# Cross attention in a two-layer encoder step: each head's query projection in two halves of 128 features

## The chip, the cores and the metric

One core of a Trainium2 chip runs the whole step in one launch. The metric is the device time of one execution in microseconds. In the profile PE is TensorE (matmuls and transposes; the array runs its instructions in the order of its list), DVE is VectorE, ACT is ScalarE, POOL is GpSimd, SP issues the loads and stores.

## What is computed

Two layers for a prompt of 512 tokens and a sample of 32 tokens; 1024 features, each layer a mixer (differential attention and a gated part), cross attention with 4 heads of 256 features into 256 memory tokens, and a convolutional feed-forward part. The change lies in the cross attention:

```python
def mem_kv(mem, norm_g, wk, wv, kg):
    m = rmsnorm(mem, norm_g)
    k = rmsnorm((m @ wk).reshape(B, M, X_HEADS, X_DH), kg)
    v = (m @ wv).reshape(B, M, X_HEADS, X_DH)
    return k, v

def cross_attend(h, mk, mv, wq, wo, qg):
    q = rmsnorm((h @ wq).reshape(B, S, X_HEADS, X_DH), qg)
    s = jnp.einsum('bqhd,bkhd->bhqk', q, mk,
                   preferred_element_type=jnp.float32) * (X_DH ** -0.5)
    p = jax.nn.softmax(s, axis=-1)
    o = jnp.einsum('bhqk,bkhd->bqhd', p.astype(mv.dtype), mv).reshape(B, S, D_MODEL)
    return o @ wo
```

The prompt attends to memory keys and values computed here, the sample to cached ones.

## The kernel before

Prompt and sample stand side by side as 544 columns (`T`), in two PSUM tiles of 272. Every large product is made of three matmuls per block of 128 x 128 weights, high part by high, high by low and low by high, in a 32-bit format whose rounded high part and remainder are kept apart (`split`: ACT casts the high part, DVE subtracts it).

Weights come as a list of items (`build_units`), and the code must take them (`pop`) in the order of that list. An item is loaded by SP into one of two staging tiles `raw` and converted into a pair of tiles `hl` (ACT the high part, L192; DVE the rest, L193), eight tiles in all, so four items. A head's query weights `wq` are two items here, 512 input rows by 256 columns each.

The cross attention of a head h is, in the order of the code: `do_mem_k` (keys from wk: PSUM tile `pm`; squares and their sums; a reciprocal root on POOL, `rmk`; the scaled keys `mk` on DVE; transposes `pmk` on PE; the cached keys' transposes `pcmk`), `do_cross_q` (queries, PSUM tiles `pqa` and `pqb` in `proj_fm`, L353, 48 matmuls for each 128 features; squares `xsq`; their sums by a small product `pqs`; the reciprocal root on POOL, `rqy`, and from it `rq` and `nrq` on DVE), `do_cross_scores` (scores `pxS`, L940, 24 matmuls in two halves of 12; their maxima `xmx` on DVE; the exponentials `P` on ACT, L949; the division on DVE, L953; the transposes `pxT` of `P`, L960, split by ACT and DVE into `pT`; for the sample the scores `pxs`, L967, which take a PSUM bank that the first half of `pxS` has, and the transposes `pxsT`, L979), `do_mem_v` (values from wv, again `pm`, then `mv` and its split `mvs`), `do_cross_out` (`pxo` and `pxso`, the results `co`). For head 0 the queries come ahead of the keys. After the four heads wo's projection (`pwca`, `pwcb`, in the same `proj_fm`) adds to the residual; the part that takes heads 0 to 2 can run before the last head's result is there.

PSUM has four banks for `pm`, `pq` and `pwc`, two for `pxS` and `pxs`, two for the transposes and `pxo`.

The code is written in this order, but the order on each engine is not: a scheduler of the tile framework sets it at build time, by its own estimate of when each instruction can start, and mixes what is written one behind the other. Each engine then runs its own list in order and waits where a semaphore isn't there yet.

Of the kernel before, what the change touches and what calls it, by code (L numbers as in the profile page):

```python
# [10 lines left out]
F32R = mybir.dt.float32r  # L11
I32 = mybir.dt.int32
AF = mybir.ActivationFunctionType
# [14 lines left out]
T = 544  # L28
S0 = 512
TH = T // 2  # L30
# [6 lines left out]
def encoder_step(ctx: ExitStack, tc: tile.TileContext, a, o):  # L37
# [20 lines left out]
    def G(tag, shape, name, dt=F32):  # L58
        return gp.tile(shape, dt, tag=tag, bufs=GB[tag], name=name)

    def tmp(shape, name, tag="t", bufs=5, dt=F32):
        return tp.tile(shape, dt, tag=tag, bufs=bufs, name=name)
# [28 lines left out]
    for i in range(NP):  # L91
        q = i // PART - 1
# [7 lines left out]
    def build_units():  # L100
        def ks(src, k0, n):
            return src[k0 * 128:(k0 + n) * 128].rearrange("(k p) c -> p k c", p=128)

        def item(tag, what, ids, n):
            items.append((tag, what, ids, n))
            for r in ids:
                raws[r][2] = len(items) - 1

        def raw(loads, nk, cols, kind="raw"):
            raws.append([loads, nk, None, cols, kind])  # L110
            return len(raws) - 1

        def two(tag, mat, cols):
            for k0 in (0, 4):
                c0, loads = 0, []
                for c, n in cols:
                    loads.append((0, 4, c0, n, ks(mat[:, c:c + n], k0, 4)))
                    c0 += n
                item(tag, None, (raw(loads, 4, 256),), 4)

        for l in range(DEPTH):
            wi = a["w_in"][l]
            kq = lambda h: two(f"kq{h}", wi, [(512 + 128 * h, 128), (128 * h, 128)])
            v_ = lambda j: two(f"v{j}", wi, [(1024 + 256 * j, 256)])
            u_ = lambda j: two(f"u{j}", wi, [(1536 + 256 * j, 256)])
            gv = lambda j: two(f"gv{j}", wi, [(2048 + 256 * j, 256)])
            for f, i in ((kq, 0), (v_, 0), (kq, 1), (kq, 2), (v_, 1), (kq, 3), (gv, 0), (u_, 0), (gv, 1), (u_, 1)):
                f(i)
            for j in range(4):
                src = a["w_out"][l][:, 256 * j:256 * j + 256].rearrange("(b q k p) c -> q b p k c", b=2, q=2, p=128)  # L130
                for q in range(2):
                    item(f"wout{j}", None, (raw([(2 * b, 2, 0, 256, src[q, b]) for b in range(2)], 4, 256),), 4)
            for h in range(4):
                for nm in ("wq", "wk") if h == 0 else ("wk", "wq"):
                    two(f"{nm}{h}", a[nm + "_c"][l], [(256 * h, 256)])
                two(f"wv{h}", a["wv_c"][l], [(256 * h, 256)])
            for j in range(4):
                two(f"wo{j}", a["wo_c"][l], [(256 * j, 256)])

            ids = None  # L140
            for what, i, j in PLAN:
                if what != "d":
                    c0 = 256 * i + 128 * j + (FF if what == "u" else 0)
                    item(f"{what}{i}_{j}", None, (raw([(0, 8, 0, 128, ks(a["w_up"][l][:, c0:c0 + 128], 0, 8))], 8, 128),), 8)
                    continue
                jj, m = j // 7, j % 7
                if m == 0:
                    src = a["w_down"][l][256 * PART * i:256 * PART * (i + 1), 256 * jj:256 * jj + 256].rearrange(
                        "(k e p) c -> e p k c", e=2, p=128)
                    ids = [raw([(0, PART, 0, 256, src[e])], PART, 256, "rawb") for e in range(2)]  # L150
                item(f"d{i}_{jj}", SEVEN[m], ids, PART)
                raws[ids[0]][2] = min(raws[ids[0]][2], len(items) - 1 - max(0, m - 3))
            for j in range(4):
                n = NF - 2 * PART * NB
                item(f"dp{j}", None, (raw([(0, n, 0, 256, ks(a["w_down"][l][:, 256 * j:256 * j + 256], NF - n, n))], n, 256),), n)
# [71 lines left out]
    def pop(tag, n=2):  # L227

        for i in state.pop("done", ()):
            state["held"] -= cost(i)  # L230
        i = state["popped"]
        prefetch()
        res = []
        for j in range(i, i + n):
            assert items[j][0] == tag, (items[j], tag)
            res.append(wt.pop(j))
        state["popped"] = i + n
        state["done"] = range(i, i + n)
        return res
# [20 lines left out]
    def split(hi, lo, src):  # L260
        act.copy(hi, src)
        vec.tensor_tensor(out=lo, in0=src, in1=f32(hi), op=ALU.subtract)
# [36 lines left out]
    def halves(ps):  # L299
        return [(ps[i][:, 0:nn], n0, nn) for i, (n0, nn) in enumerate(NSPL)]  # L300

    def psR2(name, n=0):
        f = psS if n % 3 == 2 else psR
        return [f(name + "a"), f(name + "b")]
# [42 lines left out]
    def proj_fm(ps, col, parts):  # L347

        for hl, ks, first, last in parts:
            for j, (kk, rh, rl) in enumerate(ks):  # L350
                for wpart, mv, st in ((0, rh, True), (0, rl, False), (1, rh, False)):
                    for n0, nn in NSPL:
                        pe.matmul(out=ps[0 if n0 == 0 else 1][:, 0:nn],  # L353
                                  lhsT=hl[wpart][:, kk, col * 128:col * 128 + 128],
                                  rhs=mv[:, n0:n0 + nn],
                                  start=first and j == 0 and st,
                                  stop=last and j == len(ks) - 1 and wpart == 1)

    def x_parts(w2):
        return [(w2[i], [(j, hx[:, 4 * i + j, 0], hx[:, 4 * i + j, 1]) for j in range(4)], i == 0, i == 1)  # L360
                for i in range(2)]
# [526 lines left out]
        split(mv[:, 0], mv[:, 1], m)  # L888
        return mv

    def do_cross_q(l, h, ve):
        w2 = pop(f"wq{h}")
        q = []
        qs = tmp([128, 2, 32], "qs", tag="qs", bufs=2)
        sqs = []
        for dc in range(2):
            ps = psR2("pq")
            proj_fm(ps, dc, x_parts(w2))
            qt = G("v", [128, 2, T], "xq", F32R)
            sq = tmp([128, T], "xsq")  # L900
            for v, n0, nn in halves(ps):
                split(qt[:, 0, n0:n0 + nn], qt[:, 1, n0:n0 + nn], v)
            for v, n0, nn in halves(ps):
                act.activation(out=sq[:, n0:n0 + nn], in_=v, func=AF.Square)
            act.copy(qs[:, dc], ps[1][:, S0 - TH:T - TH])
            q.append(qt)
            sqs.append(sq)
        pool.tensor_tensor(out=sqs[0], in0=sqs[0], in1=sqs[1], op=ALU.add)
        ps = psB("pqs")
        for t in range(4):  # L910
            pe.matmul(out=ps[:, 2 * t:2 * t + 2], lhsT=sqs[0][:, 128 * t:128 * t + 128], rhs=ones[:, 0:2],
                      start=True, stop=True)
        pe.matmul(out=ps[0:SS, 8:10], lhsT=sqs[0][:, S0:T], rhs=ones[:, 0:2], start=True, stop=True)
        vq = tiny([128, 5], "vq")
        pool.memset(vq, 1.0)
        vec.scalar_tensor_tensor(out=vq[:, 0:4], in0=ps[:, 0:8].rearrange("p (t j) -> p t j", j=2)[:, :, 0],
                                 scalar=1.0 / 256, in1=ve[:, 0:4], op0=ALU.mult, op1=ALU.add)
        vec.scalar_tensor_tensor(out=vq[0:SS, 4:5], in0=ps[0:SS, 8:9], scalar=1.0 / 256, in1=ve[0:SS, 4:5],
                                 op0=ALU.mult, op1=ALU.add)
        r = rsq(vq, 128, 5, "rq", pool)  # L920
        rq = tiny([128, 5], "rq16")
        nrq = tiny([128, 5], "nrq16")
        vec.tensor_scalar(out=rq, in0=r[:, 0:5], scalar1=1.0 / 16, scalar2=None, op0=ALU.mult)
        vec.tensor_scalar(out=nrq, in0=r[:, 0:5], scalar1=-1.0 / 16, scalar2=None, op0=ALU.mult)
        return q, qs, rq, nrq
# [263 lines left out]
    for l in range(DEPTH):  # L1189
# [49 lines left out]
        mt, rm, vm = do_memT(l)  # L1239
        _, ve, _ = x_stats(False)  # L1240
        co = []
        for h in range(4):
            if h == 0:
                qq = do_cross_q(l, h, ve)
            mk, cmT = do_mem_k(l, h, mt, vm)
            if h > 0:
                qq = do_cross_q(l, h, ve)
            pT, pTs = do_cross_scores(h, mk, cmT, qq)
            mv = do_mem_v(l, h, mt, rm)
            for dc in range(2):  # L1250
                t = G(COTAGS[2 * h + dc], [128, 2, T], "co", F32R)
                co.append(t)
            do_cross_out(l, h, mv, pT, pTs, co)
# [58 lines left out]
```

## Time and profile before

| | |
|---|---|
| median of 3 executions | 1649.12 us |
| lowest, highest | 1648.03 us, 1649.99 us |
| the profiled execution | 1648.65 us |
| its span in the trace | 1646.6 us |
| PE busy | 1619.5 us, 98% of the span |
| DVE, ACT, POOL busy | 1149.7 us (70%), 778.6 us (47%), 536.2 us (33%) |

The profiled execution lies 0.47 us under the median, and 2.05 us of it lie outside the span. The share of busy time is over the whole program; the cross attention of the first layer lies at about 255 to 400 us, that of the second at 1070 to 1210 us.

### The profile page before, as it was taken

To read this page: it belongs to the slowest core of one execution; us is meant where nothing else is said; L and a number is where in the kernel's file an instruction comes from. 1 tells how busy PE (TensorE), PEld (TensorE's weight loads), DVE (VectorE), ACT (ScalarE), POOL (GpSimd) and SP (SyncE) were. 2 spreads that over 40 slices of the span, in tenths; PEclk is the share of its full clock that TensorE was granted. 3 is DMA by queue.
4 is the path that set the end of the run, shared out by engine and by line. 5 is a ranking of instruction groups with operands and counts; after the bars stand their busy time and mean duration, and the time that the engine had idled before them with its cause. 6 is when DMAs were issued, how large, how long until landed. Compare 5 with 4: busy or idle time off the path is not lost.

```text
span 1646.6 us, 33007 instructions
## 1 busy us (share of the span) xinstructions
PE 1619.5 (98%) x12897; PEld 1591.7 (97%) x12897; DVE 1149.7 (70%) x2453; ACT 778.6 (47%) x1625; POOL 536.2 (33%) x910
## 2 busy tenths in 40 slices
PE   8999999999999999999999999999999999999998
PEld 8999999899999999999999999999999999999998
DVE  7778765655477777877768777655555777778774
ACT  6657744554344334343445685545543433343332
POOL 2110042222244654543321000422222545555440
PEclk9999999999999999999999999999999999999999
DMA  7322224332322332323342212243422323323322
GB/s 215 96 80 81 86 83 142 106 119 91 90 78 74 91 106 81 103 75 97 111 123 63 90 55 91 90 129 109 135 84 78 90 81 91 95 82 93 91 81 82
DMA packets 217633, 158.06 MB, mean 96 GB/s; under 512 B 8414, under 2 KB 216166, under 8 KB 217478
## 3 DMA queue, kind: packets, MB, share of 16 engines
q1 hardware_dynamic: 217414, 155.82, 31.2%
q8 instruction: 101, 1.65, 0.4%
q14 instruction: 54, 0.44, 0.1%
q10 hardware_dynamic: 64, 0.14, 0.0%
HBM read 144.83 MB, written 11.10 MB: 95 GB/s over the span
## 4 chain that ended last, share of the span: by engine, by line
PE 93%; DVE 2%; ACT 2%; POOL 2%; issue 1%; DMA 1%; ACTq 0%; SPq 0%; DVEq 0%; POOLq 0%
PE pfga L353 8%; PE pfgb L353 8%; PE pfua L353 8%; PE pfub L353 8%; PE p7a L1084 6%; PE pr L370 4%; PE pr L372 4%; PE pr L371 4%; PE p7c L1084 3%; PE pwoa L353 3%; PE pwca L353 3%; PE pqb L353 3%; PE pwob L353 3%; PE pqa L353 3%; PE pwcb L353 3%; PE pm L372 2%
## 5 line engine op out<-in xcount | busy, mean ns | idle before, releaser
L193 DVE TENSOR_TENSOR hl<-raw,hl 128x1024 fp32r<-128x1024 f32 x216 | 279.7, 1296 | 93.8 <-ACT hl L192 89.5
L192 ACT CAST hl<-raw 128x1024 fp32r<-128x1024 f32 x216 | 226.6, 1049 | 164.4 <-PE pm L371 37.5
L353 PE MATMUL pfga<-hx,hl 128*128 128x272 f32 x1056 | 264.5, 287 | 0.0
L353 PE MATMUL pfgb<-hx,hl 128*128 128x272 f32 x1056 | 264.4, 287 | 0.0
L353 PE MATMUL pfua<-hx,hl 128*128 128x272 f32 x1056 | 259.9, 288 | 3.0 <-DVE gb L1024 3.0
L353 PE MATMUL pfub<-hx,hl 128*128 128x272 f32 x1056 | 259.7, 287 | 0.0
L353 PEld LDWEIGHTS pfua<-hx,hl 128*128 128x128 f32 x1056 | 195.6, 188 | 3.2 <-DVE gb L1024 3.2
L353 PEld LDWEIGHTS pfga<-hx,hl 128*128 128x128 f32 x1056 | 198.5, 188 | 0.0
L353 PEld LDWEIGHTS pfgb<-hx,hl 128*128 128x128 f32 x1056 | 198.4, 188 | 0.0
L353 PEld LDWEIGHTS pfub<-hx,hl 128*128 128x128 f32 x1056 | 195.5, 188 | 0.0
L370 PE MATMUL pr<-hl,hx 128*128 128x256 f32 x512 | 145.6, 285 | 0.7 <-DVE zvs L413 0.7
L371 PE MATMUL pr<-hl,hx 128*128 128x256 f32 x512 | 146.0, 286 | 0.0
L372 PE MATMUL pr<-hl,hx 128*128 128x256 f32 x512 | 145.5, 285 | 0.0
L1084 PE MATMUL p7a<-at,hl 128*128 128x272 f32 x864 | 121.8, 287 | 0.0
L1084 PEld LDWEIGHTS p7a<-at,hl 128*128 128x128 f32 x864 | 113.3, 188 | 0.0
L210 ACT CAST hl<-S 128x384 fp32r<-128x384 f32 x96 | 48.4, 512 | 113.0 <-POOL S L200 40.9
L370 PEld LDWEIGHTS pr<-hl,hx 128*128 128x128 f32 x512 | 98.2, 192 | 1.4 <-DVE zvs L413 1.2
L372 PEld LDWEIGHTS pr<-hl,hx 128*128 128x128 f32 x512 | 97.0, 190 | 0.4
L371 PEld LDWEIGHTS pr<-hl,hx 128*128 128x128 f32 x512 | 97.1, 190 | 0.3
L210 ACT CAST hl<-raw 128x384 fp32r<-128x384 f32 x72 | 36.6, 511 | 108.3 <-PE pfub L353 60.9
L353 PE MATMUL pwca<-co,hl 128*128 128x272 f32 x384 | 87.5, 289 | 0.0
L353 PE MATMUL pwcb<-co,hl 128*128 128x272 f32 x384 | 87.1, 288 | 0.0
(393 smaller groups left out, 4201.6 us busy)
## 6 DMA issues: line engine op xcount, KB each, us to landing
raw<-in_w_up_dram SPq DMA_DIRECT2D x88, 512.0 KB
raw<-in_w_down_dram SPq DMA_DIRECT2D x48, 384.0 KB
raw<-in_w_in_dram SPq DMA_DIRECT2D x24, 512.0 KB
raw<-in_w_in_dram SPq DMA_DIRECT2D x32, 256.0 KB
raw<-in_w_out_dram SPq DMA_DIRECT2D x32, 256.0 KB
raw<-in_wq_c_dram SPq DMA_DIRECT2D x16, 512.0 KB
raw<-in_wk_c_dram SPq DMA_DIRECT2D x16, 512.0 KB
raw<-in_wv_c_dram SPq DMA_DIRECT2D x16, 512.0 KB
```

The lines of the kernel that those rows point to most:

```text
L192: act.copy(hi, src)
L193: vec.tensor_tensor(out=lo, in0=src, in1=f32(hi), op=ALU.subtract)
L210: act.copy(hl[:, 0], src)
L353: pe.matmul(out=ps[0 if n0 == 0 else 1][:, 0:nn], lhsT=hl[wpart][:, kk, col * 128:col * 128 + 128], rhs=mv[:, n0:n0 + nn], start=first and ...
L370: pe.matmul(out=out, lhsT=lh(k), rhs=hl[0][:, k % 4], start=(k == 0), stop=False)
L371: pe.matmul(out=out, lhsT=lh(k), rhs=hl[1][:, k % 4], start=False, stop=False)
L372: pe.matmul(out=out, lhsT=ll(k), rhs=hl[0][:, k % 4], start=False, stop=(k == k8 - 1))
L1084: pe.matmul(out=ps, lhsT=w[:, wpart, k], rhs=mv[:, part], start=fresh and k == 0 and wpart + part == 0, stop=k == PART - 1 and wpart == 1, ...
```

## The change

Each head's query weights become two items of 1024 input rows by 128 columns, one for each half of the head's features, and `do_cross_q` becomes `cross_q_half` (one half's matmuls, split and squares) and the rest. The list of weights and the code put the first half of head h + 1 between the scores of head h and the projection of its values; the second half comes where the whole projection stood.

```diff
@@ -131,8 +131,18 @@
                 for q in range(2):
                     item(f"wout{j}", None, (raw([(2 * b, 2, 0, 256, src[q, b]) for b in range(2)], 4, 256),), 4)
             for h in range(4):
-                for nm in ("wq", "wk") if h == 0 else ("wk", "wq"):
-                    two(f"{nm}{h}", a[nm + "_c"][l], [(256 * h, 256)])
+                def wq(hh, dc):
+                    c0 = 256 * hh + 128 * dc
+                    item(f"wq{hh}_{dc}", None, (raw([(0, 8, 0, 128, ks(a["wq_c"][l][:, c0:c0 + 128], 0, 8))], 8, 128),), 8)
+
+                if h == 0:
+                    wq(0, 0)
+                    wq(0, 1)
+                two(f"wk{h}", a["wk_c"][l], [(256 * h, 256)])
+                if h > 0:
+                    wq(h, 1)
+                if h < 3:
+                    wq(h + 1, 0)
                 two(f"wv{h}", a["wv_c"][l], [(256 * h, 256)])
             for j in range(4):
                 two(f"wo{j}", a["wo_c"][l], [(256 * j, 256)])
@@ -888,23 +898,28 @@
         split(mv[:, 0], mv[:, 1], m)
         return mv
 
-    def do_cross_q(l, h, ve):
-        w2 = pop(f"wq{h}")
-        q = []
-        qs = tmp([128, 2, 32], "qs", tag="qs", bufs=2)
-        sqs = []
-        for dc in range(2):
-            ps = psR2("pq")
-            proj_fm(ps, dc, x_parts(w2))
-            qt = G("v", [128, 2, T], "xq", F32R)
-            sq = tmp([128, T], "xsq")
-            for v, n0, nn in halves(ps):
-                split(qt[:, 0, n0:n0 + nn], qt[:, 1, n0:n0 + nn], v)
-            for v, n0, nn in halves(ps):
-                act.activation(out=sq[:, n0:n0 + nn], in_=v, func=AF.Square)
-            act.copy(qs[:, dc], ps[1][:, S0 - TH:T - TH])
-            q.append(qt)
-            sqs.append(sq)
+    def cross_q_half(h, dc, half):
+
+        w, = pop(f"wq{h}_{dc}", 1)
+        if dc == 0:
+            half = ([], tmp([128, 2, 32], "qs", tag="qs", bufs=2), [])
+        q, qs, sqs = half
+        ps = psR2("pq")
+        proj_fm(ps, 0, [(w, [(k, hx[:, k, 0], hx[:, k, 1]) for k in range(8)], True, True)])
+        qt = G("v", [128, 2, T], "xq", F32R)
+        sq = tmp([128, T], "xsq")
+        for v, n0, nn in halves(ps):
+            split(qt[:, 0, n0:n0 + nn], qt[:, 1, n0:n0 + nn], v)
+        for v, n0, nn in halves(ps):
+            act.activation(out=sq[:, n0:n0 + nn], in_=v, func=AF.Square)
+        act.copy(qs[:, dc], ps[1][:, S0 - TH:T - TH])
+        q.append(qt)
+        sqs.append(sq)
+        return half
+
+    def do_cross_q(h, half, ve):
+
+        q, qs, sqs = half
         pool.tensor_tensor(out=sqs[0], in0=sqs[0], in1=sqs[1], op=ALU.add)
         ps = psB("pqs")
         for t in range(4):
@@ -1239,13 +1254,17 @@
         mt, rm, vm = do_memT(l)
         _, ve, _ = x_stats(False)
         co = []
+        half = cross_q_half(0, 0, None)
         for h in range(4):
+
             if h == 0:
-                qq = do_cross_q(l, h, ve)
+                qq = do_cross_q(h, cross_q_half(h, 1, half), ve)
             mk, cmT = do_mem_k(l, h, mt, vm)
             if h > 0:
-                qq = do_cross_q(l, h, ve)
+                qq = do_cross_q(h, cross_q_half(h, 1, half), ve)
             pT, pTs = do_cross_scores(h, mk, cmT, qq)
+            if h < 3:
+                half = cross_q_half(h + 1, 0, None)
             mv = do_mem_v(l, h, mt, rm)
             for dc in range(2):
                 t = G(COTAGS[2 * h + dc], [128, 2, T], "co", F32R)
```

The scheduler sets the instructions anew. Three places, as the lists of the engines have them.

PE, the last head of layer 0, from the end of wo's first matmuls to the results: before, five `pm` and 53 `pwca` or `pwcb` stand between the scores and `pxs`, of which the last 17 are the first row here.

```order
L353 MATMUL pwca<-co,hl 128x272 x17
L967 MATMUL pxs<-cmT,qs 32x256 x2
L353 MATMUL pwca<-co,hl 128x272
L960 MATMUL pxT<-ident,P 128x128 x6
L353 MATMUL pwcb<-co,hl 128x272 x6
L960 MATMUL pxT<-ident,P 128x128 x2
L353 MATMUL pwcb<-co,hl 128x272 x12
L979 MATMUL pxsT<-ident,zvs 128x128 x2
L992 MATMUL pxo<-pT,mvs 128x512 x12
L353 MATMUL pwca<-co,hl 128x272 x2
```

The same place of the change, from the sums of squares `pqs` on; here the scores and all that stands before `pxs` are in the piece.

```order
L926 MATMUL pqs<-ones,xsq 128x2 x4
L928 MATMUL pqs<-ones,xsq 32x2
L955 MATMUL pxS<-mkT,xq 128x256 x16
L363 MATMUL pwca<-co,hl 128x272 x9
L982 MATMUL pxs<-cmT,qs 32x256 x2
L975 MATMUL pxT<-ident,P 128x128 x4
L363 MATMUL pwcb<-co,hl 128x272 x18
L975 MATMUL pxT<-ident,P 128x128 x4
L994 MATMUL pxsT<-ident,zvs 128x128 x2
L1007 MATMUL pxo<-pT,mvs 128x512 x12
L363 MATMUL pwca<-co,hl 128x272 x2
```

Between the scores and `pxs` stand nine `pwca`; the other `wo` matmuls that need no last head stand further up, among `pmk`, `pcmk` and the first scores, and 18 behind `pxs`. Between the last `pxT` and `pxo` stands `pxsT` alone, where 12 `pwcb` stood. In layer 1 this piece is the same but for how the `pxT` are grouped.

PE, head 0 of layer 0, at `pxs`. Before (the scores and six query matmuls stand right ahead):

```order
L353 MATMUL pqa<-hx,hl 128x272
L353 MATMUL pqb<-hx,hl 128x272
L967 MATMUL pxs<-cmT,qs 32x256 x2
L960 MATMUL pxT<-ident,P 128x128 x6
L353 MATMUL pqa<-hx,hl 128x272 x18
L960 MATMUL pxT<-ident,P 128x128 x2
L353 MATMUL pqa<-hx,hl 128x272 x6
L979 MATMUL pxsT<-ident,zvs 128x128 x2
L992 MATMUL pxo<-pT,mvs 128x512 x12
L353 MATMUL pqb<-hx,hl 128x272 x21
```

The change (the 16 last scores and nine `pm` stand right ahead, the last of them in the first row):

```order
L382 MATMUL pm<-hl,memT 128x256
L982 MATMUL pxs<-cmT,qs 32x256 x2
L975 MATMUL pxT<-ident,P 128x128 x4
L363 MATMUL pqa<-hx,hl 128x272 x21
L363 MATMUL pqb<-hx,hl 128x272
L975 MATMUL pxT<-ident,P 128x128 x2
L363 MATMUL pqb<-hx,hl 128x272
L975 MATMUL pxT<-ident,P 128x128 x2
L363 MATMUL pqb<-hx,hl 128x272 x19
L363 MATMUL pqa<-hx,hl 128x272
```

The query matmuls of head 1 (the first half; `pqa`, `pqb`) now stand behind `pxs` and the first `pxT`, and more of them ahead of the last `pxT` and `pxsT`.

POOL, the two reciprocal roots of head 0 in layer 0, `rq` for the queries and `rmk` for the memory keys. Before, they run mixed:

```order
L256 TENSOR_SCALAR rqt<-rqt 128x5
L247 TENSOR_SCALAR rmky<-mss 128x2
L249 TENSOR_SCALAR rmkh<-mss 128x2
L257 TENSOR_TENSOR rqy<-rqt,rqy 128x5
L251 TENSOR_TENSOR rmkt<-rmky 128x2
L251 TENSOR_TENSOR rqt<-rqy 128x5
L252 TENSOR_TENSOR rmkt<-rmkt,rmkh 128x2
L252 TENSOR_TENSOR rqt<-rqt,rqh 128x5
L256 TENSOR_SCALAR rmkt<-rmkt 128x2
L256 TENSOR_SCALAR rqt<-rqt 128x5
```

In the change the first ends before the second begins (its last four rows and the next ones):

```order
L261 TENSOR_TENSOR rqt<-rqy 128x5
L262 TENSOR_TENSOR rqt<-rqt,rqh 128x5
L266 TENSOR_SCALAR rqt<-rqt 128x5
L267 TENSOR_TENSOR rqy<-rqt,rqy 128x5
L257 TENSOR_SCALAR rmky<-mss 128x2
L259 TENSOR_SCALAR rmkh<-mss 128x2
L261 TENSOR_TENSOR rmkt<-rmky 128x2
L262 TENSOR_TENSOR rmkt<-rmkt,rmkh 128x2
```

DVE's `rq` and `nrq`, which take the first root, now stand ahead of the instruction that makes the second root's input.

## Rows read from the trace of the kernel before

**Rows 1.** The page, part 4: shares of the chain that ended last, by engine.

```profile
PE 93%; DVE 2%; ACT 2%; POOL 2%; issue 1%; DMA 1%; ACTq 0%; SPq 0%; DVEq 0%; POOLq 0%
```

**Rows 2.** Stretches: from:to, length, busy per engine (instructions), granted clock, DMA share, GB/s.

```profile
0.00:10.00 10.00, 5.11 (x24) 4.79 (x24) 5.29 (x9) 5.16 (x8) 4.59 (x23) 1.00 0.86 240
...
284.00:320.00 36.00, 34.01 (x263) 31.97 (x263) 20.13 (x46) 16.80 (x42) 8.84 (x31) 1.00 0.36 119
...
354.00:389.00 35.00, 35.00 (x274) 33.66 (x274) 19.32 (x43) 18.72 (x43) 10.05 (x31) 1.00 0.38 117
```

**Rows 3.** PE's waits: line, releaser: us in total, times, longest.

```profile
PE pxT L960 <- DVE P L953: 1.4, 2, 0.7
PE pxs L967 <- ACT P L949: 1.3, 2, 0.7
...
PE pxsT L979 <- DVE pT L262: 1.1, 2, 0.5
...
PE pxo L992 <- DVE pT L262: 0.6, 4, 0.2
...
PE pmk L858 <- DVE mk L852: 0.4, 1, 0.4
```

**Rows 4.** Timeline of PE, head 0, layer 0: start, us, instruction, idle before.

```profile
288.25 2.06 PE L940 MATMUL pxS<-mkT,xq 128*128 128x256 f32 x16
...
291.66 1.05 PE L967 MATMUL pxs<-cmT,qs 128*32 128x256 f32 x4 [0.60 <-ACT P L949]
```

**Rows 5.** Timeline of DVE, last head of layer 0.

```profile
383.46 0.69 DVE L944 TENSOR_REDUCE xmx<-pxS 128x2 f32<-128x512 f32 x1 [0.69 <-PE pxS L940]
...
385.98 1.26 DVE L193 TENSOR_TENSOR hl<-raw,hl 128x1024 fp32r<-128x1024 f32 x1 [0.86 <-ACT hl L192]
387.64 0.17 DVE L923 TENSOR_SCALAR rq<-rqy 128x5 f32<-128x5 f32 x1 [0.40 <-POOL rqy L257]
...
389.61 0.62 DVE L953 TENSOR_SCALAR P<-P,xri 128x256 f32<-128x256 f32 x2
...
395.11 1.29 DVE L262 TENSOR_TENSOR pT<-pxT,pT 128x512 fp32r<-128x512 f32 x2
```

**Rows 6.** Timeline of POOL, head 0 of layer 0: the roots' first and last instruction, 29 in all.

```profile
270.64 1.11 POOL L247 TENSOR_SCALAR rqy<-vq 128x5 int32<-128x5 int32 x1 [4.23 <-DVE vq L918]
...
279.96 0.20 POOL L257 TENSOR_TENSOR rmky<-rmkt,rmky 128x2 f32<-128x2 f32 x1
```

**Rows 7.** Timeline of POOL, last head of layer 0.

```profile
382.86 0.20 POOL L247 TENSOR_SCALAR rqy<-vq 128x5 int32<-128x5 int32 x1 [0.67 <-DVE vq L918]
...
386.25 1.08 POOL L256 TENSOR_SCALAR rqt<-rqt 128x5 f32<-128x5 f32 x1
387.41 0.20 POOL L257 TENSOR_TENSOR rqy<-rqt,rqy 128x5 f32<-128x5 f32 x1
```

**Rows 8.** Timeline of PE, last head of layer 0.

```profile
382.45 1.93 PE L940 MATMUL pxS<-mkT,xq 128*128 128x256 f32 x14
...
384.81 0.29 PE L353 MATMUL pwca<-co,hl 128*128 128x272 f32 x1
...
389.32 2.30 PE L353 MATMUL pwca<-co,hl 128*128 128x272 f32 x17
391.55 1.05 PE L967 MATMUL pxs<-cmT,qs 128*32 128x256 f32 x4
...
392.76 0.82 PE L960 MATMUL pxT<-ident,P 128*128 128x128 f32 x6
...
394.31 1.75 PE L353 MATMUL pwcb<-co,hl 128*128 128x272 f32 x12
```

**Rows 9.** Timeline of ACT, last head of layer 0.

```profile
388.73 0.56 ACT L949 ACTIVATE P<-pxS,xmx,rq 128x256 f32<-128x256 f32 x1
...
390.36 0.85 ACT L885 ACTIVATE mv<-pm,rmy 128x256 f32<-128x256 f32 x2
...
394.49 1.07 ACT L261 CAST pT<-pxT 128x512 fp32r<-128x512 f32 x2
395.45 1.06 ACT L192 CAST hl<-raw 128x1024 fp32r<-128x1024 f32 x1
```

## The prediction

> **What bounds the kernel now.** First the chain of work that ended last [rows 1]: TensorE (PE) holds 93% of it, so an engine other than PE costs time only where PE stands still for it, and a change of order can win no more than those waits. Then the stretches of the first layer's cross attention [rows 2], with PE's busy time against their length: heads 1 to 3 (354 to 389 us is the last) have no idle PE at all, and of the 36.00 us around head 0's softmax 34.01 are busy, so about 2 us are lost there. The list of PE's waits [rows 3] says at what: the sample group's scores `pxs` wait for ScalarE's exponentials, the transposes `pxT` for VectorE's scaled `P`, `pxsT` for the split of `pT`, each twice, that is once in each layer; `pxo` waits four times 0.15 (head 0 and the last head of both layers), and `pmk` once. Without the last heads' two `pxo` (0.3) the change can win 1.4 + 1.3 + 1.1 + 0.3 + 0.4 = 4.5 us of 1648.65, and no more, since it takes no matmul, byte or conversion away. What it can lose is bounded by nothing but the cover that it uses up elsewhere.
>
> **What the change removes, adds and moves.** Nothing is removed or added: the counts of matmuls, casts, vector operations and loads are the same, and a head's query weights are two loads of 512 KB as before (8 x 128 columns each where it was 4 x 256). That the runs in memory shrink from 1 KB to 512 bytes I cost at nothing: the DMA share in these stretches is 0.36 to 0.38 [rows 2], with two staging buffers between. So the sum is one of waits, made stage by stage in the new order against the durations of the old trace.
>
> Head 0. Before, 16 `pxS` start at 288.25 and `pxs` at 291.66 [rows 4], after only six query matmuls, with 0.60 us idle. The first half of `pxS` ends at about 288.25 + 8 x 0.12 = 289.2, so the way over the maxima and two exponentials to `pxs` is 2.45 us. The diff writes 48 query matmuls behind the scores; but in the order that the scheduler makes of it nine `pm` stand there, and the queries come behind `pxs` (second excerpt). PE has 8 x 0.12 + 9 x 0.12 = 2.0 us of work against the 2.45, plus 0.6 because both reductions over the scores, 0.69 us each [rows 5], now stand ahead of both small products: a stall of 1.0 in place of 0.6. With an `hl` conversion (1.26 us [rows 5]) in the way it is 2.2, with none of these it is 0.4. Behind it the 21 query matmuls need the bank that a square on ScalarE releases (0.35, an estimate: one activation of the 0.56 that an exponential takes, less what PE does meanwhile), and `pxT`, `pxsT` and `pxo` then have 22 and more matmuls of 0.125 us ahead of them, more than their waits of 0.7, 0.5 and 0.15: those go.
>
> Head 0's keys give back some. GpSimd makes two reciprocal roots there, for the queries and for the memory keys; before, they are interleaved, from 270.64 to 280.16 [rows 6], 9.5 us, and now one stands wholly behind the other (third excerpt). One chain alone takes 387.61 - 382.86 = 4.75 us with one instruction of 1.08 instead of about 0.2 in it [rows 7], so 3.9 without. Two in a row, three such long instructions (as the interleaved stretch had, an estimate from these rows), 0.4 ahead, 0.55 for VectorE's turn between and 0.45 for the first `mk`: 0.4 + 7.8 + 2.6 + 0.55 + 0.45 = 11.8 us from the end of `pqs` to `pmk`. PE has 11 `pm`, 32 query and 48 `pm` matmuls there, 91 at 0.12 to 0.125, which is 11.05: a stall of about 0.8, where layer 0 had 0.4 and layer 1 none; with no long instruction it is nothing. Head 0 in all: 1.0 + 0.35 + 0.1 + 0.8 = 2.25 per layer against 2.4 and 2.1. I put it at nothing, between -2.2 (all waits gone) and +1.5 (the conversion in the way and the keys late).
>
> Heads 1 and 2. 16 or more scores and 52 to 56 `pm` stand between `pqs` and `pxs`, 8.2 us, against a chain of at most 6.84 (worked out below), much as before: nothing.
>
> The last head is where the sum is made. There is no next head to take a half from, so what hides its softmax is the part of `wo`'s projection that needs heads 0 to 2 alone: 72 matmuls. Before, `pqs` ends and the last scores start at 382.45; 14 `pxS`, five `pm` and then 53 `pwca`/`pwcb` from 384.81 run until `pxs` at 391.55 [rows 8], 9.1 us. The other chain from the same 382.45: GpSimd's root until 387.61 [rows 7], VectorE's `rq` from 387.64 [rows 5], the second exponential until 388.73 + 0.56 = 389.29 [rows 9]. That is 6.84 us, 2.3 less than PE's work, so it is free. In the new order the wv projection of this head is over earlier (the query half that stood last now stands ahead of it), the scheduler has spent most of the 72 matmuls around `pmk` and the first scores, and between `pqs` and `pxs` remain 16 `pxS` and nine `pwca` (first excerpt): 16 x 0.12 + 9 x 0.125 = 3.0 us (the pitches from [rows 8]: 19 in 382.45 to 384.81, 53 from there to 391.55). Step by step from `pqs`:
> - The chain is 6.84, or 6.0 without the one long GpSimd instruction, which lies inside the conversion on VectorE at 385.98 [rows 5, 7]; that conversion now stands behind, so I take 6.0. `pxs` stalls 6.0 - 3.0 = **2.95** (3.8 with the long one).
> - `pxs` takes 1.0. The scaled `P` is there (390.23 - 382.45 - 0.86 = 6.9 [rows 5]). After four `pxT` of about 0.1 [rows 8] PE is at 7.35, and 18 `pwcb` need the bank that the second `mv` on ScalarE frees: 391.21 in the old frame [rows 9], so 7.9. Stall **0.5**.
> - The 18 end at 10.2, four `pxT` at 10.6. Then nothing is left: `pxsT` and `pxo` follow at once, where 12 `pwcb` stood before. ScalarE has a weight cast (1.06) ahead of its two `pT` (1.07 together) [rows 9], and the cast waits for the 11th of the 18, so it ends at 10.35; the `pT` run from 10.7 to 11.25 and 11.8. VectorE has its own conversion (1.26) ahead of its `pT` (1.29 together) [rows 5]; it ends at 11.6, the two `pT` at 12.3 and 12.9. `pxsT` stalls 12.3 - 10.6 = **1.7**, `pxo` **0.4**.
>
> Together 5.55 per layer, less the 0.15 that was there: 5.4. Without the conversions ahead it would be 4.5, with the long instruction on GpSimd and later conversions 6.8. Both layers have this order: 2 x 5.4 = 10.8. The order changes also in the second layer's mixer, by a few places; I see no wait in it and give it nothing, within 2 us either way. The matmuls run are the same, so the stall has no counterpart in saved work; work moved ahead of `pmk` only fills places that were full before.
>
> Sum: 1648.65 + 10.8 + 0 = 1659.5. The profiled execution stands 0.47 below the median, 1649.12; on the median's side it is 1660.
>
> **Rivals.** A difference under 0.2%, 3.3 us, can hardly be told from none.
> - The waits only trade places: head 0 hides all five of its waits (-4.5) and each tail pays only for `pxs` (2 x 2.95): 1650, no measurable change. For it: the 48 matmuls are in the right neighbourhood. Against it: the nine `pm` and the empty tail of the new order. 0.12.
> - Faster: the last head's reciprocal root on GpSimd is the one price that decides. Were its 4.3 to 5.2 us [rows 7] so much shorter, or started so much ahead of the scores, that the tails pay under 2.25 each, head 0's 4.5 would win; with a free tail it is 1644.2. Against it: in both orders `pqs` stands right before the 16 (14) scores, and the chain starts with it. 0.06.
> - The order on PE is another but every wait stays as long, for instance because the moved `wo` matmuls free PE for the same length later: 1648.7. Against it: PE runs its list in order and all of it is busy in 354 to 389 [rows 2]. 0.05.
> - The clock. In the first 10 us PE is busy for 5.11 alone, and the granted clock is 1.00 there, as in the other stretches [rows 2]: 2.4 GHz, no fall. Should the tail's stalls, several of them within 10 us, make it fall to 1.2 GHz, the about 7 us of PE work between `pqs` and `pxo` would take up to 7 us more in each layer: 1674. 0.05. The Trainium skill, "TensorE: Matmul & The Clock Gate", Part 1: The HAM clock gate, says that the throttled state is the default and that activity releases it, so a PE that idles falls back to half. By that rule this change, which makes holes in a stretch that had none, would be punished twice; the trace, with 1.00 in the stretch that holds its longest idle time, does not bear it out here.
>
> **How the numbers follow.** The forecast has 0.72, with its own range of 1653 (tails 4.5, head 0 gaining 2.2, or the mixer 2 better) to 1667 (tails 6.8, head 0 losing 1.5, and the mixer's 2 in part). The range for 8 in 10 reaches down to the rival at 1650 and up to 1667; the 1644, the 1648.7 and the 1674 stay outside with 0.16, and a little of the forecast's own ends. Faster by over 0.2%: 0.08 (the faster rival and a little of the first). Within 0.2%: 0.18 (most of the first, the third, the lowest end of the forecast). Slower: 0.74.
>
> **What will show it.** Right: PE's list of waits has `pxs` from ScalarE's `P` four times, near 1 us in the head 0s and near 3 us in the last heads, `pwcb` on `mv` at 0.5, `pxsT` on `pT` at 1.7 in the last heads only, and PE no longer fully busy in the last head's stretch; the granted clock stays 1.00. Wrong: a `pxs` of the last head without a wait (the chain from `pqs` is then shorter than in this trace), head 0's `pxs` stall of 2 us or none, a new wait of the query projections for their weights (`hl` from a load that now stands behind another in SP's queue), or waits in the second layer's mixer that were not there before.

## The result, and the profile after

The changed kernel takes 1662.72 us (median of 5, 1662.11 to 1664.05) against 1648.99 us before: ratio 1.0082, 95% interval 1.0070 to 1.0093. It is slower, as forecast, and inside the range; the forecast was 1660. The profiled execution of the change, the longest of the five, took 1664.05 us with a span of 1662.3, 15.7 more than before.

PE's waits in the change (us in total, times, longest), the rows that answer to [rows 3]:

```profile
PE pxs L982 <- ACT P L964: 9.4, 4, 2.9
...
PE pxsT L994 <- DVE pT L272: 3.2, 2, 1.7
...
PE pmk L868 <- DVE mk L862: 1.5, 2, 0.7
...
PE pxo L1007 <- DVE pT L272: 0.3, 2, 0.2
PE pwcb L363 <- ACT mv L895: 0.2, 1, 0.2
```

They sum to 14.6 us where [rows 3] have 4.8: 9.8 more. `pxT`'s wait is gone, `pxs` has four waits instead of two, up to 2.9. All other waits together changed by 0.3. So about 6 us of the 15.7 are not waits: PE's busy time grew by 6.0, from 1619.5 to 1625.5 us, with as many instructions as before.

PE's timeline in the last head of layer 0 (start, us, instruction, idle before), the answer to [rows 8]:

```profile
388.46 2.17 PE L955 MATMUL pxS<-mkT,xq 128*128 128x256 f32 x16
390.48 1.28 PE L363 MATMUL pwca<-co,hl 128*128 128x272 f32 x9
394.62 1.05 PE L982 MATMUL pxs<-cmT,qs 128*32 128x256 f32 x4 [2.86 <-ACT P L964]
...
396.44 3.88 PE L363 MATMUL pwcb<-co,hl 128*128 128x272 f32 x18 [0.16 <-ACT mv L895]
```

and, behind four more `pxT`:

```profile
402.30 0.44 PE L994 MATMUL pxsT<-ident,zvs 128*128 128x128 f32 x2 [1.54 <-DVE pT L272]
402.90 4.61 PE L1007 MATMUL pxo<-pT,mvs 128*128 128x512 f32 x12 [0.16 <-DVE pT L272]
```

Only nine `pwca` stand between the scores and `pxs`, and PE is idle 2.86 us there; `pxsT` waits 1.54. The durations changed too: 18 `pwcb` take 3.88 us, 0.21 each, where [rows 8] have 0.125 to 0.13, and 12 `pxo` take 4.61, where the run `fill` below has 3.06. The stretches of 2 us say why (length; busy time and instructions of PE, of its weight loads, of DVE, ACT and POOL; then the granted clock, the DMA share, GB/s):

```profile
392.00:394.00 2.00, 0.00 (x0) 0.00 (x0) 0.47 (x4) 0.64 (x3) 0.61 (x3) 1.00 0.00 0
394.00:396.00 2.00, 1.38 (x8) 0.76 (x8) 1.08 (x4) 2.00 (x9) 0.18 (x1) 1.00 0.00 0
396.00:398.00 2.00, 1.84 (x10) 1.58 (x9) 1.77 (x7) 1.53 (x5) 0.81 (x1) 0.53 0.37 119
398.00:400.00 2.00, 2.00 (x12) 2.00 (x12) 0.74 (x2) 0.68 (x2) 0.00 (x0) 0.62 0.06 21
400.00:402.00 2.00, 0.76 (x7) 0.53 (x5) 1.58 (x2) 1.46 (x3) 0.00 (x0) 1.00 0.00 0
402.00:404.00 2.00, 1.54 (x5) 1.11 (x6) 1.00 (x3) 0.00 (x0) 0.00 (x0) 0.73 0.56 156
404.00:406.00 2.00, 2.00 (x6) 1.56 (x5) 0.00 (x0) 0.14 (x1) 0.00 (x0) 0.50 0.30 107
```

The granted clock falls from 1.00 to about 0.5 twice, that is from 2.4 to 1.2 GHz: at 396, behind the stretch in which PE did nothing (392 to 394), and at 403, behind `pxsT`'s wait. Before, it was 1.00 in 354 to 389 us [rows 2], and in 389 to 430 too. Layer 1's last head in the change:

```profile
1215.36 1.91 PE L982 MATMUL pxs<-cmT,qs 128*32 128x256 f32 x4 [2.87 <-ACT P L964]
1217.21 1.12 PE L975 MATMUL pxT<-ident,P 128*128 128x128 f32 x4
1217.97 2.83 PE L363 MATMUL pwcb<-co,hl 128*128 128x272 f32 x18
...
1222.93 0.44 PE L994 MATMUL pxsT<-ident,zvs 128*128 128x128 f32 x2 [1.69 <-DVE pT L272]
1223.53 3.04 PE L1007 MATMUL pxo<-pT,mvs 128*128 128x512 f32 x12 [0.16 <-DVE pT L272]
```

`pxs` takes 1.91 instead of 1.05 here, behind 2.87 us of idle PE; the later `pxo` has its full speed (3.04).

### The profile page after: what moved, and what is told of

The parts are those of the page before. It is cut to its first block, busy times and chain, and to the rows that moved or that the text cites. A ratio compares the mean times of both kernels' runs of the same rounds, so it can differ in the third digit from the quotient of the medians.

```text
span 1662.3 us, 32989 instructions
## 1 busy us (share of the span) xinstructions
PE 1625.5 (98%) x12897; PEld 1595.1 (96%) x12897; DVE 1145.2 (69%) x2453; ACT 775.4 (47%) x1625; POOL 539.5 (32%) x910
## 4 chain that ended last, share of the span: by engine, by line
PE 89%; DVE 3%; ACT 2%; DMA 2%; POOL 2%; issue 1%; SPq 1%; ACTq 0%; DVEq 0%; POOLq 0%
PE pfga L363 8%; PE pfgb L363 8%; PE pfua L363 7%; PE pfub L363 7%; PE p7a L1099 6%; PE pr L380 3%; PE pr L382 3%; PE pr L381 3%; PE p7c L1099 3%; PE pwcb L363 3%; PE pwob L363 3%; PE pwoa L363 3%; PE pwca L363 3%; PE pqa L363 3%; PE pqb L363 3%; PE p7b L1099 2%
## 5 line engine op out<-in xcount | busy, mean ns | idle before, releaser
L210 POOL TENSOR_TENSOR S<-raw 128x384 f32<-128x384 f32 x48 | 59.4, 1238 | 100.4 <-DMA raw<-in_w_down_dram 61.7
```

The source lines that it names most:

```text
L210: pool.tensor_tensor(out=t, in0=in0, in1=in1, op=op)
```

## Experiments

The theory after these rows is called A in the expectations: the change takes 48 matmuls from in front of the last head's softmax and puts them in head 0; PE then runs out of work before the chain from `pqs` over GpSimd's reciprocal root to the second exponential has ended, and behind such stalls PE's clock falls. There are two rivals: B, that the cut of the weights into 128 columns costs by itself; and that the lower clock has another cause than the stalls. Ratios are to the kernel before, run on the same chip in the same round; the last column is the mean granted clock over the span, lowest and highest of the executions (0.999 to 1.000 for the kernel before, beside the runs).

| run | wo matmuls before the last `pxs` | median us | ratio, 95% interval | mean clock |
|---|---|---|---|---|
| the change | 9 | 1662.72 | 1.0082 [1.0070, 1.0093] | 0.995 to 0.996 |
| early2 | 22 | 1658.34 | 1.0055 [1.0040, 1.0070] | 0.998 to 1.000 |
| early1 | 37 | 1655.94 | 1.0035 [1.0022, 1.0048] | 0.997 to 1.000 |
| split_only | 53 | 1653.37 | 1.0024 [1.0014, 1.0033] | 0.998 to 0.999 |
| qfirst3 | 17, root earlier | 1655.02 | 1.0034 [1.0022, 1.0045] | 0.997 to 1.000 |
| fill | 9 and 24 of no use | 1657.12 | 1.0044 [1.0030, 1.0058] | 0.999 to 1.000 |
| fill_a | 9 and 24 of no use | 1659.88 | 1.0061 [1.0044, 1.0078] | 0.996 to 0.999 |
| fill_b | 9 | 1659.13 | 1.0056 [1.0041, 1.0071] | 0.997 to 1.000 |

The intervals of neighbouring versions overlap. What tells them apart is the waits in their profiles.

**The halves moved for fewer heads.** `split_only` cuts the weights the new way and moves nothing, `early1` moves head 1's first half alone, `early2` those of heads 1 and 2. The edit of `early2` (with 1 and 0 for 2 in the other two):

```diff
-                if h < 3:
+                if h < 2:
                     wq(h + 1, 0)
...
+            if h > 2:
+                half = cross_q_half(h, 0, None)
             if h > 0:
                 qq = do_cross_q(h, cross_q_half(h, 1, half), ve)
...
-            if h < 3:
+            if h < 2:
                 half = cross_q_half(h + 1, 0, None)
```

(and `wq(h, 0)` in the list of weights ahead of `wq(h, 1)` for the heads that are not moved.)

> Both halves of each head stand where the whole projection stood; only the weights' items and loads are cut the new way. Theory A (cover: what counts is how many matmuls stand between pqs and pxs in the last head, and what runs at the lower clock behind a stall): 53 wo matmuls stand there again, so no wait of pxs in the last heads, granted clock 1.00, 1648 to 1651 us (head 0's pxs has no query matmul ahead in layer 0, which costs about 0.7). Theory B (the split itself costs: 512-byte runs, other items and conversions): 1655 or more.

> Only head 1's first half is moved ahead of head 0's values. 37 wo matmuls stand between the last head's scores and pxs. Theory A: 16 x 0.12 + 37 x 0.125 = 6.5 us against a chain of 6.2, so no wait of pxs there; pxsT still has nothing in front and waits 1.6 per layer; head 0 as in the change (2.3 to 2.9 per layer). Waits of the cross attention 8 to 9 us against 4.7, little or no time at the lower clock in the tails: 1652 to 1655. Theory B: as slow as the change, 1660 or more. Rival on the clock (it falls wherever the new order stands, whatever the stall): a fall in the tails here too.

> Heads 1 and 2 have their first half moved, head 3 not. 22 wo matmuls stand between the last head's scores and pxs. Theory A: 16 x 0.12 + 22 x 0.125 = 4.7 us against 6.2: pxs waits 1.4 to 1.5, pxsT 1.6; waits 11 to 12 us in all, 1655 to 1657 without a fall of the clock, up to 1661 if the tails fall as they do in the change. Theory B: 1660 to 1664.

PE in the last head of layer 0; first `early2`:

```profile
386.31 2.17 PE L957 MATMUL pxS<-mkT,xq 128*128 128x256 f32 x16
...
388.81 2.40 PE L365 MATMUL pwca<-co,hl 128*128 128x272 f32 x18
392.43 1.05 PE L984 MATMUL pxs<-cmT,qs 128*32 128x256 f32 x4 [1.21 <-ACT P L966]
...
398.89 0.44 PE L996 MATMUL pxsT<-ident,zvs 128*128 128x128 f32 x2 [1.70 <-DVE pT L274]
399.49 4.60 PE L1009 MATMUL pxo<-pT,mvs 128*128 128x512 f32 x12 [0.16 <-DVE pT L274]
```

then `early1`:

```profile
393.92 1.05 PE L984 MATMUL pxs<-cmT,qs 128*32 128x256 f32 x4
...
400.15 0.44 PE L996 MATMUL pxsT<-ident,zvs 128*128 128x128 f32 x2 [1.91 <-DVE pT L274]
```

then `split_only`:

```profile
394.46 1.05 PE L984 MATMUL pxs<-cmT,qs 128*32 128x256 f32 x4
```

`pxs` waits 2.86, 1.21, 0 and 0 us with 9, 22, 37 and 53 matmuls ahead: 16 scores and 22 matmuls last 6.12 - 1.21 = 4.9 us in `early2`'s rows (386.31 to 392.43), and 37 are enough. Behind `early2`'s `pxsT` the clock fell in layer 0 (`pxo` 4.60), in layer 1 it did not; its time lies between the two that were expected, for no fall and for falls as in the change. `pxsT` waits 1.5 to 1.9 wherever nothing stands between the last `pxT` and it, and not in `split_only`'s last heads, where 12 `pwcb` do. So the cover, the work that PE has while the chain runs, is shown as the cause of the waits in the last heads.

The expectations' times were too low for `early1` and `split_only`. In `early1` new waits in the middle heads, which I had not worked out, came in: four of `pqb` for ScalarE's `xsq`, 0.8 each. In `split_only` it is head 0: in layer 0 its `pxs` has no query matmul ahead, and waits 3.6 where 0.7 was expected. PE there:

```profile
294.29 1.05 PE L984 MATMUL pxs<-cmT,qs 128*32 128x256 f32 x4 [3.57 <-ACT P L966]
```

and VectorE ahead of it:

```profile
289.73 1.22 DVE L205 TENSOR_TENSOR hl<-raw,hl 128x1024 fp32r<-128x1024 f32 x1 [1.51 <-ACT hl L204]
290.88 0.68 DVE L961 TENSOR_REDUCE xmx<-pxS 128x2 f32<-128x512 f32 x1
291.48 0.43 DVE L274 TENSOR_TENSOR xq<-pqa,xq 128x272 fp32r<-128x272 f32 x1
291.83 0.43 DVE L274 TENSOR_TENSOR xq<-pqb,xq 128x272 fp32r<-128x272 f32 x1
292.18 0.68 DVE L961 TENSOR_REDUCE xmx<-pxS 128x2 f32<-128x512 f32 x1
```

VectorE does an `hl` conversion ahead of the two reductions `xmx` that `pxs` waits for, and two splits of `xq` between them (the 16 scores start at 288.66). So B holds in a part that was not meant by it: the cut alone is 0.24% slower, but no wait of PE is put down to a load or a conversion, and the last heads are as before. What the rows show in their place is the order that the scheduler makes of other items in head 0: 3.6 us there, with a granted clock of 0.95 in 285 to 320 us, and 0.7, 1.7 and 1.0 at `pxs`, `pqa` and `pxsT` in layer 1. With `pxo` these waits are 7.6 us against the 4.8 of [rows 3], and PE is busy for 1.7 more: 4.5 of the 4.8 by which the span grew. No run changes that order alone.

**What the stalls' matmuls cost at the lower clock.** `fill` is the changed kernel with work whose results nobody reads: 24 matmuls of the scores' kind ahead of the last head's `pxs`, and 18 transposes of `P` ahead of its `pxsT`. The order of all else is as in the change.

```diff
+        if h == 3:
+            for j in range(2):
+                fill = psB("fill")
+                for n in range(12):
+                    pe.matmul(out=fill[:, 0:256], lhsT=q[1][:, 1, 384:512], rhs=mk[:, 0, 1], start=n == 0,
+                              stop=n == 11)
         pT = []
...
+        if h == 3:
+            fill = psS("fill2")
+            for n in range(18):
+                pe.transpose(fill[:, 128 * (n % 4):128 * (n % 4) + 128], P[1][:, 1, 128:256], ident)
         pt = psB("pxsT")
```

> The changed kernel, with work added that nobody reads: in the last head 24 matmuls of the scores' kind ahead of pxs and 18 transposes of P ahead of pxsT, where PE stands idle 2.9 and 1.6 us. Theory A: the waits are filled, not shortened, so they save nothing by themselves; the granted clock stays 1.00 in both tails and pwcb, pxo and pxs run at their 0.125, 0.235 and 0.25 pitch again: about 4.5 us less than the change, 1657 to 1659. If the lower clock was not the stalls' doing, the same time as the change or up to 1 us more: 1662 to 1664.

PE in the last head of layer 0:

```profile
388.26 2.17 PE L955 MATMUL pxS<-mkT,xq 128*128 128x256 f32 x16
390.27 3.04 PE L975 MATMUL fill<-mkT,xq 128*128 128x256 f32 x24
...
394.40 1.05 PE L988 MATMUL pxs<-cmT,qs 128*32 128x256 f32 x4
...
396.22 2.51 PE L363 MATMUL pwcb<-co,hl 128*128 128x272 f32 x18 [0.18 <-ACT mv L895]
...
399.00 2.13 PE L1001 MATMUL fill<-ident,P 128*128 128x128 f32 x18
400.97 0.38 PE L1004 MATMUL pxsT<-ident,zvs 128*128 128x128 f32 x2
401.45 3.06 PE L1017 MATMUL pxo<-pT,mvs 128*128 128x512 f32 x12
```

`pxs` starts 6.14 us after the scores, as in the change (6.16): the added work shortened nothing. But `pwcb` takes 2.51 instead of 3.88 and `pxo` 3.06 instead of 4.61, the granted clock is 1.00 in every stretch of the cross attention, and the kernel is faster than the change: it lies 7.4 us above its own before, the change 13.7 above its own, so about 6 us are saved, at a time that was expected (1657 to 1659). That is not the luck of one execution: all five of the change have a mean granted clock of 0.995 or 0.996, all five of `fill` 0.999 or 1.000. One stall is left: head 0's `pxs` in layer 1 still waits 2.1 us, with no fall behind it in this profile; in `fill_a`'s, with the same wait, there is one (0.95 in 1100 to 1135 us).

**One gap filled at a time.** `fill_a` has the first of the two additions, `fill_b` the second.

> As fill, but only the first gap of the last heads (ahead of pxs) holds the added matmuls; the wait of pxsT (1.6) stays. If each long stall brings the clock down by itself, the first fall's cost goes in both layers (1.5 and 1.9 us by the changed kernel's rows) and the second may stay: 1658 to 1660. If the 1.6 us wait is too short to bring it down without the first: as fill, 1656 to 1658.

> As fill, but only the second gap (ahead of pxsT) holds the added transposes; the wait of pxs (2.9) stays. The first fall stays in both layers, the second of layer 0 (1.9 us) goes: 1660 to 1662. If the first stall were not what brings the clock down: below 1659.

PE in the last heads, first `fill_a` in layer 1:

```profile
1218.11 0.44 PE L1000 MATMUL pxsT<-ident,zvs 128*128 128x128 f32 x2 [1.70 <-DVE pT L272]
1218.70 4.61 PE L1013 MATMUL pxo<-pT,mvs 128*128 128x512 f32 x12 [0.16 <-DVE pT L272]
```

then `fill_b` in layer 0:

```profile
394.12 1.05 PE L982 MATMUL pxs<-cmT,qs 128*32 128x256 f32 x4 [2.83 <-ACT P L964]
...
395.95 2.52 PE L363 MATMUL pwcb<-co,hl 128*128 128x272 f32 x18 [0.18 <-ACT mv L895]
```

`fill_a` lies where it was expected if each long stall can bring the clock down: behind 1.70 us of wait `pxo` takes 4.61 in layer 1 (in layer 0, behind the same wait, the granted clock stayed at 1.00). `fill_b` came out faster than expected, just above the 1659 under which the first stall was not to count. Its profiled execution shows why the expectation was too simple: 2.83 us of wait, and `pwcb` at full speed behind it, in both layers. This execution is the fastest of its four (1657.19 us, mean clock 1.000); the other three took 1659.04 to 1660.25 at 0.997 and 0.998. In the change's profiled execution such a wait was followed by 1.2 GHz in both layers. So a stall of this length can be followed by a fall, and need not be. What either gap costs by itself these two runs do not tell, since their intervals overlap.

**The root ahead of the keys.** `qfirst3` is the change with the last head's second half taken ahead of its keys, so that its reciprocal root starts earlier:

```diff
+            if h == 3:
+                qq = do_cross_q(h, cross_q_half(h, 1, half), ve)
             mk, cmT = do_mem_k(l, h, mt, vm)
-            if h > 0:
+            if h > 0 and not (h == 3):
                 qq = do_cross_q(h, cross_q_half(h, 1, half), ve)
```

(the list of weights likewise.)

> The changed kernel, with the last head's second half taken ahead of its keys instead of behind them, so that pqs stands a key projection's time before the scores. Only 17 wo matmuls stand between the last head's scores and pxs. If the chain that decides is the reciprocal root on GpSimd that starts at pqs (theory A), it is long over when the scores come; what is left is maxima and two exponentials, 2.5 to 3.1 us against 8 x 0.12 + 17 x 0.125 = 3.1: pxs waits 0 to 0.3 in the last heads, though early2 with 22 matmuls waited 1.2. pxsT still waits about 1.7, head 2's pxs 0.5 to 0.8 (16 scores and 28 matmuls, 5.4 us). 1653 to 1657 us. If only the number of matmuls behind the scores counts, pxs waits 1.8 and the time is 1659 or more.

PE in the last head of layer 0:

```profile
390.10 2.30 PE L365 MATMUL pwca<-co,hl 128*128 128x272 f32 x17
392.33 1.05 PE L984 MATMUL pxs<-cmT,qs 128*32 128x256 f32 x4
...
398.56 0.44 PE L996 MATMUL pxsT<-ident,zvs 128*128 128x128 f32 x2 [1.91 <-DVE pT L274]
```

17 matmuls now cover `pxs` fully, where 22 left 1.21 in `early2`. GpSimd's root is done at 387.34 here, before the last 16 scores start at 388.20. So it is the root's 4.3 us that the last head has to hide, and not the softmax behind the scores alone. Head 2 pays for the half that it lost (`pxs` waits 1.4 there, beside head 0's 1.1), and `pxsT` still waits 1.9. Of the six executions, the two with a mean granted clock of 1.000 took 1652.6 and 1652.7 us, the four with 0.997 to 0.999 took 1654.2 to 1657.6: one order, with and without falls.

No version here beats the kernel before.

## Why the prediction was right, and where it was not

- **The bound, and nothing removed.** Right: what changed is waits of PE and its clock. PE's instructions are as many as before.
- **Last head, `pxs`.** 2.95 was forecast, 2.86 and 2.87 came. GpSimd's root in the last head of layer 0 has no long instruction, as chosen:

```profile
388.88 0.20 POOL L257 TENSOR_SCALAR rqy<-vq 128x5 int32<-128x5 int32 x1 [2.14 <-DVE vq L933]
...
392.58 0.20 POOL L267 TENSOR_TENSOR rqy<-rqt,rqy 128x5 f32<-128x5 f32 x1
```

  From the scores' start at 388.46 to the root's end at 392.78 is 4.3 us; the second exponential ends at 394.5, and `pxs` starts at 6.16 where 6.0 was worked out.
- **Last head, the rest.** `pwcb` 0.16 for 0.5, `pxsT` 1.54 and 1.69 for 1.7, `pxo` 0.16 for 0.4. `pwcb` waits in layer 0 alone. Together 4.7 per layer for 5.55: the terms were each on the high side, `pwcb`'s most, since PE came later to it than worked out (it waits from 396.44 - 0.16 = 396.28, 7.8 after the scores' start, for 7.35).
- **Head 0.** 1.0 was forecast at `pxs` and 2.2 named as the case with a conversion in the way; the conversion is in the way, and the wait is 1.59 in layer 0 and 2.08 in layer 1. VectorE in layer 0:

```profile
289.95 1.23 DVE L203 TENSOR_TENSOR hl<-raw,hl 128x1024 fp32r<-128x1024 f32 x1 [3.46 <-ACT hl L202]
291.10 1.28 DVE L959 TENSOR_REDUCE xmx<-pxS 128x2 f32<-128x512 f32 x2
```

  Both reductions (1.28) start only when `hl` is done, and the wait of `pqa` for `xsq` (0.35) did not come. `pmk` waits 0.72 for 0.8. Head 0 in all 2.3 and 2.8, for 2.25: close to the 2.4 and 2.1 of before, as the "nothing" of the sum had it.
- **The step that failed: the clock.** It was a rival of 0.05, and its cost in the sum was nothing. The rows of low clock in the change, against the same instructions in `fill`: 3.88 - 2.51 and 4.61 - 3.06 in layer 0's last head, 2.9; in layer 1's last head 1.91, 1.12 and 2.83 against 1.05, 0.66 and 2.51, 1.6; the same, 1.6, in layer 1's head 0, behind 2.08 us of wait:

```profile
1112.98 1.92 PE L982 MATMUL pxs<-cmT,qs 128*32 128x256 f32 x4 [2.08 <-ACT P L964]
1114.83 1.12 PE L975 MATMUL pxT<-ident,P 128*128 128x128 f32 x4
1115.59 3.20 PE L363 MATMUL pqa<-hx,hl 128*128 128x272 f32 x21
```

  (1.05 and 0.66 at 2.4 GHz, and 21 matmuls 2.89 in layer 0.) Together 6.2 us, beside the 6.0 by which PE's busy time grew. The sign that the granted clock stays 1.00 did not come.

  The rival was dismissed on the strength of the first 10 us, whose granted clock is 1.00 beside 4.9 us of idle PE [rows 2]. That row was misread. PE's timeline of before has the same instruction twice near it:

```profile
13.21 1.91 PE L1174 MATMUL pxin<-ident,xin 128*128 128x128 f32 x8
...
16.55 1.03 PE L1174 MATMUL pxin<-ident,xin 128*128 128x128 f32 x8
```

  Eight transposes take 1.91 us and then 1.03, and the `pr` matmuls start 0.21 us apart from 10.65 to 13.0, and 0.12 apart from 15.73 on: until then PE ran at 1.2 GHz. The trace has no record of the clock before 15.66 us, and the column shows 1.00 there. So the kernel before had the lower clock behind its longest idle time, too. The rows from 396 and 404 us show it behind the stalls of the change (0.53 and 0.50). The Trainium skill, "TensorE: Matmul & The Clock Gate", Part 1: The HAM clock gate, has the throttled state as the default, to which an idle TensorE returns. These rows agree with it, where the prediction had held the 1.00 against it.

  That the stalls are the cause is shown by `fill` for the last heads, 4.5 of the 6.2 us. For head 0's 1.6 no run fills the stall, and the cause is argued from the same pattern. What decides in a given execution whether a stall of 1.5 to 2.9 us is followed by a fall is open.

The time was forecast 2.7 us too low, and the profiled execution 4.5 (1659.5 for 1664.05). The waits came out 1.0 us smaller than worked out, and 6 us of clock were not in the sum at all; the first offsets little of the second. That the result still lies inside the range is luck in this part: the range was made wide for the waits, not for the clock. The rival at 1674 had the right mechanism and too large a price: the clock stays low for part of the work behind a stall, not for all of it.

## What to carry to other kernels

Work put earlier in a loop over heads is work missing at its end: count, for the last iteration, what stands between the start of its longest chain on the slower engines and the instruction that waits for it, and read that chain's length from the trace of before. A stall of PE in dense work can cost as much again in clock as in waiting (here 1.4 to 1.6 us behind four of the six waits of 1.5 to 2.9 in the cross attention, none behind the other two), so price it by both, and look at the granted clock in short stretches behind it. Hold a granted clock of 1.00 against the durations of the same instruction elsewhere before an argument rests on it. What a scheduler makes of a rewritten loop is read from its list, not from the code: the 48 matmuls were written behind the scores and stood behind the waiting instruction.

## What the runs showed of the hardware that was not expected

Useless matmuls in the stalls made the program about 6 us faster (1.0044 of before in place of 1.0082), with a mean granted clock of 0.999 or 1.000 in every execution. Equal waits are not always followed by the lower clock: 2.86 us was in the change, 2.83 us was not in `fill_b`, and the executions of `qfirst3` differ by 5 us, with mean granted clocks of 1.000 and 0.998 (1652.64 and 1657.63). A granted clock of 1.00 in a stretch at the program's start stood beside matmuls at half their later pace (0.21 us apart, then 0.12).
